# Gains moved out of the activations, and value and gate products in blocks of 512 columns, in a one-core encoder layer

## The chip, the cores and the metric

The kernel runs on one core of a Trainium2 chip. A core has engines that run side by side, each with its own stream of instructions in a fixed order: TensorE (PE in the profile; its weight loads are listed as PEld), VectorE (DVE), ScalarE (ACT), GpSimd (POOL) and SyncE (SP, which here only starts DMA transfers). Sixteen DMA engines move data between the chip's memory and the core's own memory. Products are accumulated in PSUM, in banks of 512 four-byte numbers for each of the 128 partitions.

The metric is the device time of one execution in microseconds, as the median of several runs. An instruction waits until the instructions ahead of it on its engine have been issued, and until what it reads is there and what it overwrites is no longer needed. So the order on an engine matters as much as the durations.

## The reference

One layer of a streaming encoder: a mixer made of three kinds of heads, then a feed-forward part with a causal convolution, each between two RMS norms. There are 1024 tokens of a new stream (the prompt) and 32 of a running one (the sample).

```python
def rms_norm(x, g):
    y = xf * lax.rsqrt(jnp.mean(xf * xf, axis=-1, keepdims=True) + EPS)
    return y * g

def head_rms_norm(x, g):
    y = x * lax.rsqrt(jnp.mean(x * x, axis=-1, keepdims=True) + EPS)
    return y * g.reshape(h, d)
...
proj = xn @ w_in           # 15 parts: queries, keys, decays; values gv, hi, mv; gates gr, hg, mo
o_a = head_rms_norm(o_a, g_a) * jax.nn.silu(hs(gr, GLA_H))
o_b = head_rms_norm(o_b, g_b) * jax.nn.silu(hs(hg, HG_H))
o_c = head_rms_norm(h, g_c) * jax.nn.sigmoid(hs(mo, ML_H))
cat = jnp.concatenate([o_a, o_b, o_c])
return cat @ w_out
...
h = mixer(rms_norm(x, g_mix_pre))      # the first of the two gains in question
x = x + rms_norm(h, g_mix_post)
h = conv_ffn(rms_norm(x, g_ffn_pre))
x = x + rms_norm(h, g_ffn_post)
```

Two gains matter here: `g_mix_pre`, one number for each of the 1024 features that enter `w_in`, and `g_head` (cut into `g_a`, `g_b`, `g_c`), one number for each of the 1024 features that enter `w_out`.

## The kernel before

**Work.** The tokens go in three groups: 384, 384, and 256 prompt plus 32 sample tokens. Within a group they are cut into units of 128 (the sample tokens are a short unit). A group passes through the projections (`inproj`). The head computations of a group (`mixer`, one unit after the other: levels of decays `x`, `Ld`, `Qz`, scores `sc`, outputs `og`, `oh`) are interleaved with the projections of the next group. After the third group come the output product (`zp`, blocks of 512 columns), the up product (`pux`, `puw`, `puy`, `puz`), and the down product (`q`, `x`). The order of instructions on each engine comes from a scheduler that simulates the program when the kernel is built; the code only gives the program order and a few constraints (`issue_after`, `high_priority`).

**Precision.** Each float32 operand of a product is split in a high part (a cast: `xh`, `wt_0h`) and a low part (the rest: `xl`, `wt_0l`), and one product is three matmuls, `mm3` (L101 high by high, L102, L103).

**Into the group.** `scale_x` takes each unit's rows `x` and multiplies them on DVE with the rstd of the row and with `gx`, the gain `g_mix_pre` copied to all partitions (512 KB; L310 for the two halves of the first unit, L319). `norm_group` transposes a unit on PE in two halves of four 128-column pieces into one PSUM tile `xt` each (L330). ACT casts a half out of PSUM into `xh` (L333), DVE subtracts to make `xl` (L334).

**Order of the projections in a group.** First block 0 of the values together with 26 columns of small gates: 282 columns, `pv` of block 0, each unit 24 matmuls; then the feature-major products `pf` (13 blocks of weights `wf_8`, `wf_6`, `wf_7`, `wf_3`, ...); then the blocks 1 to 7 of values and gates, 256 columns each. For a block the weights come in two tiles `wt_0`, `wt_1` (three in block 0). In the first group the raw weights are split on the chip (ACT L107, DVE or POOL L110) and the low parts stored (`lf_d`, `lt_d`, L355). In the later groups the low parts are loaded (SP L347) and only the cast is made again (ACT L349). Weight tiles have three raw buffers, and four buffers for high and low parts.

**Out of a block.** `vg_store` copies values out of PSUM (ACT L431) and sends them to `v_d`. For gates ACT makes a tanh (L113, into `vth`, one buffer; in the third group `gth`, three), DVE combines it with the sum in PSUM (L440, L442), POOL multiplies by `gh`, the gain `g_head` on all partitions (512 KB loaded on SP's queue at L652, times 0.5 on DVE at L653; L444), and POOL sends the result to `g_d` (L445). The third group makes blocks 1 to 7 feature-major with 288 columns and transposes them back (`vg_across`).

**Output weights.** `out_weights` splits the eight tiles of `w_out` (a cast on ACT, a subtraction on DVE).

## Time and profile before

| what | before |
|---|---|
| median of 3 runs (lowest, highest) | 1357.33 us (1355.49, 1357.98) |
| span of the profiled execution | 1355.3 us |
| PE busy | 1310.8 us, 97% |
| PEld busy | 1196.7 us, 88% |
| DVE busy | 1025.2 us, 76% |
| ACT busy | 709.8 us, 52% |
| POOL busy | 317.6 us, 23% |

The profile gives the span of its execution, first to last instruction, and no separate time for that execution; the three runs lie 0.2 to 2.7 us above the span. Busy time counts an instruction from its start to its modelled end. Matmuls overlap in the array, so their busy times sum to more than the time in which they pass; the distance from start to start is what one costs. The groups list an instruction by line, engine and tile names, with the mean of one, and the idle time of its engine just ahead of it with what ended that. In the timeline a row is a run of like instructions with the start and the time they took. In tables of windows PEclk is the granted clock of TensorE as a share of full speed.

### The profile page before, as it was taken

The page shows a single profiled execution, that of the slowest core. Times are in us where ns is not written, and L with a number is a line of the kernel's source. Part 1 is how long each engine was busy: PE and PEld are TensorE (multiplying, and loading weights), DVE is VectorE, ACT ScalarE, POOL GpSimd, SP SyncE. Part 2 cuts the span into 40 slices and gives each one's busy share as a digit, 9 for nine tenths or more (in the row PEclk, how much of TensorE's full clock was granted, in tenths as well). Part 3 has the DMA queues.
Part 4 walks back from the last instruction along what each step waited for, and adds up shares of the span by engine and source line. Part 5 has one row for each costly group of instructions (what it writes and reads, how often), then busy time and mean ns, then how long its engine had stood idle before and what let it go on. Part 6 is the DMA issues. An engine that isn't in the chain of part 4 may idle for free.

```text
span 1355.3 us, 29229 instructions
## 1 busy us (share of the span) xinstructions
PE 1310.8 (97%) x11472; PEld 1196.7 (88%) x11472; DVE 1025.2 (76%) x1921; ACT 709.8 (52%) x1362; POOL 317.6 (23%) x530
## 2 busy tenths in 40 slices
PE   6999999999999999999999999999999999999997
PEld 5999889998888887767899999999999996678885
DVE  5795649768598678876998888888888876499566
ACT  5555556555574555435654554545554545454552
POOL 4532303135032254213211212111111110010005
PEclk9999999999998989989999999999999999999998
DMA  9799778886879963454315457536455239645435
GB/s 342 241 358 363 265 244 258 278 281 211 292 230 308 336 201 125 142 182 103 128 48 188 134 133 189 134 111 180 120 147 154 82 127 397 254 161 146 141 102 124
DMA packets 126881, 269.72 MB, mean 199 GB/s; under 512 B 24167, under 2 KB 59143, under 8 KB 126663
## 3 DMA queue, kind: packets, MB, share of 16 engines
q1 hardware_dynamic: 113111, 244.78, 53.2%
q0 software_dynamic: 9120, 18.62, 7.3%
q10 hardware_dynamic: 4512, 4.46, 1.0%
q8 instruction: 90, 1.47, 0.5%
q14 instruction: 48, 0.39, 0.1%
HBM read 206.72 MB, written 86.18 MB: 216 GB/s over the span
## 4 chain that ended last, share of the span: by engine, by line
PE 63%; DVE 5%; DMA 3%; ACT 3%; issue 2%; POOL 1%; SPq 0%; DVEq 0%; POOLq 0%; ACTq 0%
PE pux L103 5%; PE pux L102 5%; PE pux L101 5%; PE puw L101 3%; PE puw L103 3%; PE puw L102 3%; PE q L101 3%; PE q L102 3%; PE q L103 3%; PE x L101 2%; PE x L102 2%; PE x L103 2%; PE puz L103 2%; PE puz L101 2%; PE puz L102 2%
## 5 line engine op out<-in xcount | busy, mean ns | idle before, releaser
L1409 DVE SCALAR_TENSOR_TENSOR y<-uu,fconv_sb,y 128x1060 f32<-128x1060 f32 x88 | 116.2, 1320 | 36.8 <-ACT y L1407 36.2
L1345 ACT COPY c<-pux 128x272 f32<-128x272 f32 (+1 forms) x132 | 49.3, 375 | 50.5 <-PE pux L103 49.8
L1407 ACT ACTIVATE y<-uu,fconv_sb 128x1060 f32<-128x1060 f32 x44 | 56.1, 1275 | 8.5 <-POOL uu L1403 7.8
L101 PE MATMUL pv<-wt_0h,xh 128*128 128x256 f32 (+1 forms) x192 | 56.3, 293 | 3.6 <-DVE xl L334 1.6
L103 PE MATMUL zp<-woh,cl 128*128 128x512 f32 (+1 forms) x144 | 57.7, 401 | 1.5 <-DVE cl L1106 1.5
L1406 POOL COPY fhalo<-uu 128x2 f32<-128x2 f32 x44 | 16.6, 376 | 180.7 <-DVE uu L1350 180.6
L101 PE MATMUL zp<-woh,ch 128*128 128x512 f32 (+1 forms) x144 | 57.8, 410 | 0.8 <-ACT ch L1105 0.8
L102 PE MATMUL zp<-wol,ch 128*128 128x512 f32 (+1 forms) x144 | 57.9, 402 | 0.0
L103 PE MATMUL pv<-wt_1h,xl 128*128 128x256 f32 (+1 forms) x192 | 55.1, 287 | 0.0
L103 PE MATMUL pv<-wt_0h,xl 128*128 128x256 f32 (+1 forms) x192 | 55.0, 286 | 0.0
L102 PE MATMUL pv<-wt_0l,xh 128*128 128x256 f32 (+1 forms) x192 | 54.8, 286 | 0.0
L101 PE MATMUL pv<-wt_1h,xh 128*128 128x256 f32 (+1 forms) x192 | 54.7, 285 | 0.0
L102 PE MATMUL pv<-wt_1l,xh 128*128 128x256 f32 (+1 forms) x192 | 54.4, 283 | 0.0
L1585 POOL TENSOR_TENSOR gss<-gss 128x1 f32<-128x1 f32 (+1 forms) x9 | 8.2, 906 | 185.0 <-ACT gjk L1578 185.0
L221 POOL TENSOR_SCALAR hrs<-hss 128x5 f32<-128x5 f32 (+3 forms) x27 | 10.1, 375 | 176.5 <-DVE hss L1015 172.6
L831 DVE COPY_PREDICATED P<-masks_sb,sc 128x352 f32<-128x352 int32 (+3 forms) x53 | 37.9, 715 | 5.9 <-PE sc L744 5.0
L101 PEld LDWEIGHTS pv<-wt_0h,xh 128*128 128x128 f32 x192 | 36.4, 190 | 5.3 <-DVE xl L334 2.1
L1403 POOL COPY uu<-uu 128x2 f32<-128x2 f32 x44 | 28.0, 637 | 38.8 <-DVE uu L1350 37.8
L101 PEld LDWEIGHTS pv<-wt_1h,xh 128*128 128x128 f32 x192 | 36.2, 189 | 0.7 <-issue 0.6
L222 POOL TENSOR_TENSOR hrs<-hrs,mhalf 128x5 f32<-128x5 f32 (+3 forms) x27 | 36.2, 1341 | 2.2
L103 PEld LDWEIGHTS pv<-wt_0h,xl 128*128 128x128 f32 x192 | 36.5, 190 | 0.2
L102 PEld LDWEIGHTS pv<-wt_0l,xh 128*128 128x128 f32 x192 | 36.5, 190 | 0.1
(1743 smaller groups left out, 5321.0 us busy)
## 6 DMA issues: line engine op xcount, KB each, us to landing
wrP<-in_w_dn SPq DMA_DIRECT2D x27, 512.0 KB, 4.4
h_d<-y SPq DMA_DIRECT2D x22, 530.0 KB, 3.7
ht<-h_d SPq DMA_DIRECT2D x22, 530.0 KB, 10.5
wt_0r<-in_w_tok SPq DMA_DIRECT2D x21, 512.0 KB, 5.7
wt_1r<-in_w_tok SPq DMA_DIRECT2D x21, 512.0 KB, 6.3
ws_d<-in_w_dn POOLq DMA_DIRECT2D x20, 512.0 KB, 8.9
wrP<-ws_d SPq DMA_DIRECT2D x20, 512.0 KB, 4.0
wt_0l<-lt_d SPq DMA_DIRECT2D x14, 512.0 KB, 4.5
```

Of the source, the lines that this page charges most:

```text
L101: pe.matmul(ps, lh[0], rh[0], start=first, stop=False, **kw)
L102: pe.matmul(ps, lh[0], rh[1], start=False, stop=False, **kw)
L103: return pe.matmul(ps, lh[1], rh[0], start=False, stop=last, **kw)
L221: pool.tensor_scalar(out, ss, 1.0 / width, eps, op0=ALU.mult, op1=ALU.add)
L222: pool.tensor_tensor(out, out, mhalf[:n, :cols], op=ALU.pow)
L831: dve.copy_predicated(dst, mk.broadcast_to([n, 11, *mk.shape[2:]]), src)
L1345: kept[name] = act.copy(t, ps)
L1403: pool.tensor_copy(u[:, GAP_P:GAP_P + 2], u[:, GAP_S - 2:GAP_S])
L1406: behind["POOL"] = pool.tensor_copy(fhalo[:, j, :], u[:, NCOL - 2:NCOL])
L1407: act.activation(y, u, AF.Identity, scale=fconv[:, j, 2:3], bias=fconv[:, j, 3:4])
L1409: dve.scalar_tensor_tensor(y, uu[i][:, s:s + NCOL], fconv[:, j, s:s + 1], y, op0=ALU.mult, op1=ALU.add)
L1585: pool.tensor_tensor(ss[:n, 0:1], ss[:n, 2:3], ss[:n, 3:4], op=ALU.add)
```

## The change

- **Gain of the norm as columns.** The tile `gx` and its load go. A table `gin` of 128 by 2 by 8 numbers holds both gains by columns (8 KB, loaded on ACT's queue). Rows are multiplied by the rstd alone. After the transposes the feature lies on the partitions, so the gain is a number per partition there: for each 128-column piece ACT writes `xh` with `scale` and DVE writes `xl` with one instruction of two operations. A half that had one cast and one subtraction has four and four: 18 halves, 72 pieces.
- **Gain of the heads in the output weights.** The tile `gh`, its load and its multiplication by 0.5 go, and so do the 36 multiplications on POOL. The tanh, the combination with the PSUM sum, and the DMA to `g_d` use one tile. The casts and subtractions of `w_out` carry the gain times 0.5, in as many instructions as before.
- **Blocks of 512 columns.** In the first two groups the blocks 1 to 6 become three wide blocks (`WIDE`, numbered 1, 3 and 5) of 512 columns. A wide block has four weight tiles of two 128-row parts by 512 columns (512 KB as before). One unit's sum fills one bank. Block 7 stays at 256 columns. High and low weight tiles have five buffers instead of four. The tile out of PSUM, `vg`, is 512 columns with two buffers. The three units of two narrow blocks were 6 x 24 matmuls of 256 columns; they are now 3 x 24 of 512 columns.
- **Stored low parts.** They lie in the layout of the wide blocks (`lw_d`). The third group, whose blocks stay narrow, reads them for blocks 1 to 6 in two transfers of 256 KB with rows of 1 KB, where it had one of 512 KB with rows of 4 KB.

```diff
-    gx = p1.tile([128, 1024], F32, name="gx")
-    act.dma_start(gx, a["grows"][3:4, :].broadcast_to([128, 1024]))
+    gin = cp.tile([128, 2, 8], F32, name="gin_sb")
+    act.dma_start(gin, a["gin"])
+    gmix, ghead = gin[:, 0], gin[:, 1]
...
-                dve.scalar_tensor_tensor(x[:n], x[:n], rs[:n], gx[:n], op0=ALU.mult, op1=ALU.mult)
+                dve.tensor_scalar(x[:n], x[:n], rs[:n], None, op0=ALU.mult)
...
-                s = slice(4 * hf, 4 * hf + 4), slice(off, off + n)
                 with tc.high_priority(offset=AHEAD):
-                    act.copy(xh[(slice(None), *s)], ps[:, :, :n])
-                    dve.tensor_tensor(xl[(slice(None), *s)], ps[:, :, :n], xh[(slice(None), *s)].bitcast(F32), op=ALU.subtract)
+                    for k in range(4):
+                        c, gk = (slice(None), 4 * hf + k, slice(off, off + n)), gmix[:, 4 * hf + k:4 * hf + k + 1]
+                        act.activation(xh[c], ps[:, k, :n], AF.Copy, scale=gk)
+                        dve.scalar_tensor_tensor(xl[c], ps[:, k, :n], gk, xh[c].bitcast(F32), op0=ALU.mult, op1=ALU.subtract)
...
-    def weights(src, pool_, name, shape, tags=("wr", "wh", "wl"), bufs=(3, 4), ...
+    def weights(src, pool_, name, shape, tags=("wr", "wh", "wl"), bufs=(3, 5), ...
...
+            elif blk in WIDE and g < 2:
+                parts = [(a["w_wide"][blk // 2, c], range(2 * c, 2 * c + 2), lw_d[blk // 2, c], 512) for c in range(4)]
...
-            pool.tensor_tensor(o[:n], th[:n], gh[:n, c0:c0 + 256], op=ALU.mult)
-            pool.dma_start(g_d[t:t + n, c0:c0 + 256], o[:n])
+            pool.dma_start(g_d[t:t + n, c1:c1 + w], th)
...
-            N = 256 if blk else 282
+            N = 512 if blk in WIDE else 256 if blk else 282
...
                         mm3(ps[:n, :N], (xh[:, k, off:off + n], xl[:, k, off:off + n]), ws[k], k == 0, k == 7)
+                        if k == 3 and N == 512:
+                            yield
...
-        if g == 0:
-            sp.dma_start(gh, a["grows"][2:3, :].broadcast_to([128, 1024]))
-            dve.tensor_scalar(gh, gh, 0.5, None, op0=ALU.mult)
...
-        for blk in range(1, 8):
+        for blk in (*WIDE, 7):
             yield from vg(blk)
-            if blk == 2 and g < 2:
+            if blk == 1 and g < 2:
                 for (u, off, n) in units_of(g + 1):
                     x_in[u] = load_x(u)
...
+            act.activation(W[1][k], wo_raw[k], AF.Copy, scale=gk)
+            dve.scalar_tensor_tensor(W[2][k], wo_raw[k], gk, W[1][k].bitcast(F32), op0=ALU.mult, op1=ALU.subtract)
```

The scheduler makes a new order from this. Three places follow. In the names of these rows the first digit after a tile's name is the unit or the group: `xt20` and `xt21` are the halves of the third unit, `pv2_0` the sum of the third unit in block 0, `wf0_6r` a raw weight tile of the first group.

The first is ACT at the start of the program, from the cast of `wf_8` on, before:

```order
L107 CAST wf0_8h_349<-wf0_8r_347 128x1024
L333 CAST xh0_162<-xt20_289 128x4x128
L460 COPY tgs0_180<-pv1_0_260 128x26
L431 COPY vg1_0_286<-pv1_0_260 128x256
L333 CAST xh0_162<-xt21_296 128x4x128
L107 CAST wf0_6h_407<-wf0_6r_405 128x1024
L460 COPY tgs0_180<-pv2_0_303 128x26
L431 COPY vg2_0_329<-pv2_0_303 128x256
L107 CAST wf0_7h_445<-wf0_7r_443 128x1024
```

And now, the same place (the pieces of the second unit, `xt10` and `xt11`, stand behind the cast of `wf_8`):

```order
L108 CAST wf0_8h_386<-wf0_8r_384 128x1024
L336 ACTIVATE xh0_163<-xt10_259,gin_sb_95 128x128 x2
L108 CAST wf0_6h_442<-wf0_6r_440 128x1024
...
L336 ACTIVATE xh0_163<-xt20_314,gin_sb_95 128x128
L108 CAST wf0_7h_480<-wf0_7r_478 128x1024
L336 ACTIVATE xh0_163<-xt21_327,gin_sb_95 128x128
L108 CAST wf0_3h_518<-wf0_3r_516 128x1024
L336 ACTIVATE xh0_163<-xt21_327,gin_sb_95 128x128
L476 COPY tgs0_181<-pv2_0_340 128x26
```

Before, one half of the third unit stood behind the cast of `wf_8` and none behind those of `wf_6`, `wf_7` and `wf_3`; now pieces of the second unit stand behind `wf_8` and `wf_6`, and the last two pieces of the third unit behind `wf_7` and `wf_3`.

The second is DVE where the first group's units enter the second group's projections: `xl1` is the second group's low part, `xt30` and `xt31` the halves of its first unit; `x0`, `Ld0`, `Qz0`, `kw2`, `w0`, `P` belong to the first unit's mixer. Before:

```order
L334 TENSOR_TENSOR xl1_1709<-xt30_1711,xh1_1708 128x4x128
L865 TENSOR_TENSOR Qz0_152<-x0_8_2177,qe0_1955 128x128
L442 TENSOR_SCALAR vth2_7_1695<-vth2_7_1695 128x256
L831 COPY_PREDICATED P_161<-masks_sb_110,sc0_2_2090 128x176x2
L856 TENSOR_TENSOR Ld0_150<-x0_8_2177,k0_1816 128x32x8
L334 TENSOR_TENSOR xl1_1709<-xt31_1718,xh1_1708 128x4x128
```

Now:

```order
L337 SCALAR_TENSOR_TENSOR xl1_1471<-xt30_1473,gin_sb_95,xh1_1470 128x128
L867 TENSOR_TENSOR Ld0_152<-x0_2_1869,k0_1602 128x128x2
L872 TENSOR_TENSOR Qz0_154<-x0_2_1869,q0_1601 128x128
L457 TENSOR_SCALAR vg2_1792_1458<-vg2_1792_1458 128x256
L862 TENSOR_TENSOR x0_8_1975<-b0_1603 128x512
L842 COPY_PREDICATED P_162<-masks_sb_111,sc0_0_1778 128x22x16
L337 SCALAR_TENSOR_TENSOR xl1_1471<-xt31_1486,gin_sb_95,xh1_1470 128x128
L862 TENSOR_TENSOR x0_4_1983<-b0_1603 128x512
L337 SCALAR_TENSOR_TENSOR xl1_1471<-xt30_1473,gin_sb_95,xh1_1470 128x128
L967 TENSOR_TENSOR x0_0_1991<-q0_1601,k0_1602 128x512
L337 SCALAR_TENSOR_TENSOR xl1_1471<-xt31_1486,gin_sb_95,xh1_1470 128x128
L867 TENSOR_TENSOR Ld1_153<-x0_4_1983,k0_1602 128x64x4
```

Two subtractions with four rows between them have become eight pieces with 19 rows of mixer work between the first and the last (the rows shown hold the first four).

The third is SP's queue in the second group, where raw and low weights of the values and gates are asked for (`wt1_3_1l`: second group, block 3, tile 1, low). Before, two tiles a block:

```order
L347 DMA wt1_4_1l_3512<-lt_d_90 128x1024
L343 DMA wt1_5_1r_3647<-in_w_tok 128x1024
L343 DMA wt1_6_0r_3991<-in_w_tok 128x1024
L767 DMA vm0_158<-v_d_81 128x5x64
L773 DMA ab3_4443<-a_d_79 64x320 x2
L347 DMA wt1_5_0l_3644<-lt_d_90 128x1024
L343 DMA wt1_6_1r_3997<-in_w_tok 128x1024
L347 DMA wt1_5_1l_3650<-lt_d_90 128x1024
```

Now, four tiles a wide block:

```order
L354 DMA wt1_3_1l_3092<-lw_d_91 128x1024
L354 DMA wt1_3_2l_3098<-lw_d_91 128x1024
L346 DMA wt1_5_0r_3271<-in_w_wide 128x1024
L354 DMA wt1_3_3l_3104<-lw_d_91 128x1024
...
L354 DMA wt1_5_1l_3280<-lw_d_91 128x1024
L354 DMA wt1_5_2l_3286<-lw_d_91 128x1024
L346 DMA wt1_7_0r_3694<-in_w_tok 128x1024
L354 DMA wt1_5_3l_3292<-lw_d_91 128x1024
```

A block of the weights is still asked for tile by tile, but with five buffers and four tiles a block only one tile of the next block finds a free buffer while a block is in use; the others wait until the last unit has passed the part that held the buffer.

More of the change, by code (lines that the diff above doesn't have):

```diff
@@ L346, in weights @@
         if kept:
-            behind["low"] = sp.dma_start(l.bitcast(F32), low.bitcast(F32))
+            if len(low.shape) > 3:
+                for c in range(2):
+                    behind["low"] = sp.dma_start(l[:, 2 * c:2 * c + 2].bitcast(F32), low[c].bitcast(F32))
+            else:
+                behind["low"] = sp.dma_start(l.bitcast(F32), low.bitcast(F32))
             if heng is None:
@@ L460, in vg @@
                     act.copy(tgs[:n, i, :], ps[:n, 256:])
-                vg_store(blk, u, off, n, ps)
+                vg_store(256 * blk, N if blk else 256, u, off, n, ps)
                 yield
```

74 lines of the change are left out of this document (40 added, 34 removed).

## The prediction

> **What bounds the kernel now.** I read the page first, then PE's waits, then the timeline of PE, ACT, DVE and SP at the three places where the change acts, then windows with the clock.
>
> ```profile
> span 1355.3 us, 29229 instructions
> PE 1310.8 (97%) x11472; PEld 1196.7 (88%) x11472; DVE 1025.2 (76%) x1921; ACT 709.8 (52%) x1362; POOL 317.6 (23%) x530
> PE xt L330 <- DVE x L310: 9.7, 1, 9.7
> PE pv L101 <- DVE xl L334: 1.6, 2, 1.4
> PE pv L101 <- DVE vth L440: 1.5, 1, 1.5
> PE pv L103 <- DMA wt_1l<-lt_d: 1.2, 1, 1.2
> ```
>
> PE is the bound: 97% busy. Of the waits that the change touches (the last four rows: waited for, us in total, times, longest), the first is the start, before any data is there; the other three sum to 4.3 us. So a gain can come from matmuls that pass faster, from a shorter start, or from these few waits. POOL is 23% busy, and what it no longer does counts only where somebody waits for it.
>
> What a matmul costs is its distance to the next one, read from the timeline between the first and last row of an unbroken stretch. The first pair stands 45 matmuls of 256 columns apart, the second 12 matmuls of 512 columns.
>
> ```profile
> 94.72 0.28 PE L101 MATMUL pv<-wt_0h,xh 128*128 128x256 f32 x1
> 99.94 0.28 PE L103 MATMUL pv<-wt_0h,xl 128*128 128x256 f32 x1
> 565.08 0.39 PE L103 MATMUL zp<-woh,cl 128*128 128x512 f32 x1
> 567.81 0.39 PE L103 MATMUL zp<-woh,cl 128*128 128x512 f32 x1
> L101 PE MATMUL pv<-wt_0h,xh 128*128 128x256 f32 (+1 forms) x192 | 56.3, 293 | 3.6 <-DVE xl L334 1.6
> L103 PE MATMUL zp<-woh,cl 128*128 128x512 f32 (+1 forms) x144 | 57.7, 401 | 1.5 <-DVE cl L1106 1.5
> ```
>
> (99.94 - 94.72) / 45 = 0.116 us for 256 columns, (567.81 - 565.08) / 12 = 0.2275 us for 512. Two narrow ones cost 0.232.
>
> **Wider blocks.** Two groups, three units, three wide blocks, 24 matmuls each: 432 wide ones for 864 narrow. 432 x (0.232 - 0.2275) = 1.9 us gained. Bounds: nothing, and 4 us if a narrow one is 0.1185 in slower stretches. I take -2. The weight loads halve too, but they lie beside the matmuls (PEld overlaps PE), so I count nothing for them; in an unbroken stretch the distance of 0.116 holds what they cost. The section "Back-to-back issue gap" of the Trainium skill's page "TensorE: Matmul & The Clock Gate" gives an isolated spacing of N / 2.4 + 2.5 ns, by which 432 fixed parts of 2.5 ns go, an estimate of 1.1 us instead of my 1.9.
>
> **The start.** The rows of ACT and SP there, and of DVE and ACT for the pieces' prices:
>
> ```profile
> 12.11 0.59 ACT L333 CAST xh<-xt 128x512 fp32r<-128x512 f32 x1
> 17.46 0.19 ACT L460 COPY tgs<-pv 128x26 f32<-128x26 f32 x1
> 20.25 1.05 ACT L107 CAST wf_8h<-wf_8r 128x1024 fp32r<-128x1024 f32 x1 [2.02 <-DMA wf_8r<-in_w_feat]
> 21.67 0.18 ACT L460 COPY tgs<-pv 128x26 f32<-128x26 f32 x1
> 24.58 1.05 ACT L107 CAST wf_6h<-wf_6r 128x1024 fp32r<-128x1024 f32 x1 [1.96 <-DMA wf_6r<-in_w_feat]
> 26.48 0.18 ACT L460 COPY tgs<-pv 128x26 f32<-128x26 f32 x1 [0.86 <-PE pv L103]
> 24.20 0.38 SPq L343 DMA_DIRECT2D wf_3r<-in_w_feat  x1
> DMA to landing us min/median/max: 5.8/5.8/5.8
> 21.30:26.30 5.00, 4.56 (x42) 3.85 (x40) 2.02 (x3) 2.37 (x5) 2.90 (x2) 1.00 1.04 419
> L1210 ACT ACTIVATE xg<-fxt,gcols_sb x8: 362/384/411, 646.6 to 648.4; 128x128 f32<-128x128 f32 x8
> L861 DVE TENSOR_TENSOR Qz<-x,q x53: 174/279/981, 114.1 to 591.4; 128x128 f32<-128x128 f32 x48, 128x32 f32<-128x32 f32 x5
> L334 DVE TENSOR_TENSOR xl<-xt,xh x18: 284/688/714, 11.4 to 344.7; 128x512 fp32r<-128x512 f32 x16, 128x128 fp32r<-128x128 f32 x2
> ```
>
> The landing row is that of `wf_3r` in the first group. The copies `tgs` at 17.46, 21.67 and 26.48 mark the ends of the three units of block 0. The windows row (PE, PEld, DVE, ACT, POOL busy, clock, DMA share, GB/s) shows the DMA engines full while PE still works: loads are what the features wait for here.
>
> Loads first: 1 MB less is written (`gx`, `gh`). At the 419 GB/s of the windows row that is about 2.5 us by the time `wf_6r` comes, 1.2 us of it ahead of the first unit. So `wf_8r` can land near 17.7, `wf_6r` near 22, each instead of the cast's start at 20.25 and 24.58.
>
> Then the pieces. A half by four activations like `xg` (the only ones here out of PSUM with a scale per partition) takes 8 in 646.6 to 648.4, so about 0.26 us from start to start, 1.0 a half against 0.5 to 0.6 for the cast. On DVE I take 0.28 for a piece by the 128x128 row, 1.1 a half against 0.69. First unit: ACT now has all three weight casts ahead, then the eight pieces with the Square of the third unit between; `xl` likewise has three splits ahead and the third unit's scaling between. I put the last `xl` near 16.5, by ten of these instructions behind the loads, and the unit's end near 18, about half a microsecond later than 17.5 even with data 1.2 us sooner.
>
> Second unit: all eight `xh` pieces stand behind `wf_8`'s cast (18.7), the last six behind that of `wf_6` too (23): 23 + 0.2 for the copy + 6 x 0.26 + 0.3 for the last `xl` gives 25.1, then what matmuls are left, 26. Before, this unit was done when ACT copied its sum at 21.7. Third unit: the last two pieces stand behind the casts of `wf_7` and of `wf_3`. Before, `wf_3r` was asked for at 24.20, behind POOL's split of `wf_8`; now that split is 1.6 us sooner at the best, so `wf_3r` lands near 22.6 + 5.8 = 28.4, its cast ends at 29.4, the last piece, its `xl` and six matmuls end near 30.5. Before it was 26.3. That is +4. The features then follow PE-bound as they did, and I see no cover for this: every later matmul needs them. Bounds: -1.2 if the pieces wait for none of the casts' loads (data sooner and nothing else), +6.5 if loads are no sooner than before (then `wf_3r` lands at 30, third unit near 32.5).
>
> **First to second group.** Rows of PE, of windows (the last is the stretch in which the first new unit's halves come and its matmuls pass), and of DVE's, POOL's and ACT's groups.
>
> ```profile
> 142.63 0.58 PE L101 MATMUL pv<-wt_0h,xh 128*128 128x256 f32 x1 [1.53 <-DVE vth L440]
> 142.60:146.00 3.40, 3.37 (x15) 3.37 (x16) 3.28 (x11) 1.97 (x6) 1.45 (x2) 0.51 0.53 207
> 146.00:149.40 3.40, 3.40 (x44) 3.20 (x44) 1.78 (x8) 2.25 (x7) 1.62 (x2) 0.99 0.33 97
> L851 DVE TENSOR_TENSOR x<-b x44: 272/680/1362, 108.9 to 582.6; 128x512 f32<-128x512 f32 x40, 128x128 f32<-128x128 f32 x4
> L831 DVE COPY_PREDICATED P<-masks_sb,sc x53: 332/553/985, 145.5 to 599.2; 128x352 f32<-128x352 int32 x40, 128x704 f32<-128x704 int32 x8, 32x176 f32<-32x176 int32 x4, 32x352 f32<-32x352 int32 x1
> 153.25:160.07 6.82, 6.52 (x75) 5.80 (x72) 6.76 (x15) 3.63 (x10) 1.63 (x4) 1.00 0.98 362
> L444 POOL TENSOR_TENSOR vg<-vth,gh x24: 717/732/1656, 118.8 to 334.1; 128x256 f32<-128x256 f32 x24
> ACT vth L113: 11.7, 7
> ```
>
> Now: PE waits 1.5 us for a gate's `vth`, and right behind it the clock is at 0.51 for 3.4 us: 15 matmuls where the next window has 44. So a wait of 1.5 us cost about 1.5 + 1.7. That wait hangs on one buffer of `vth`, held until POOL's L444 has read it (0.73 us; ACT waited 11.7 us in 7 places for it). L444 is gone and there are two buffers: up to 3.2 us gained. A page rule bears on the clock: the Trainium skill ("TensorE: Matmul & The Clock Gate", "Part 1: The HAM clock gate") says that the clock halves after an idle window of about 3.4 us. The length of the slow stretch agrees; here 1.5 us of idling was enough to start one.
>
> Against it stands DVE's order. Between the first and last `xl` piece of the new unit 19 rows of mixer work now stand: 22 instructions: three level products like L851 (0.68), three `P` (L831, 0.55) and 16 others, which I take at the 0.28 of L861, the row nearest in size: 2.0 + 1.7 + 4.5 = 8.2 us, and 2 us of pieces. Each matmul group of that unit waits for its piece, and PE's order has only about 3 us of block 0 and 3 us of mixer products to put there. So 4 to 5 us idle where the stretch from 153.25 to 160.07 had 6.82 - 6.52 = 0.3, but the same mixer work is then done earlier, and I give back a third: 3 us of idling, and one slow stretch (1.7) as before. Sum 3 + 1.7 - 3.2 - 0.3 = +1.2; I take +1.5, bounds -3 (wait and slow stretch go, pieces hidden) and +5 (5 us idle and a second slow stretch).
>
> **Second to third group.** There the chain is a gate, then the transposes, then `xh` and `xl`:
>
> ```profile
> 328.98 0.66 PE L330 MATMUL xt<-ident,x 128*128 128x128 f32 x4 [0.73 <-ACT vth L113]
> 332.75 0.40 PE L101 MATMUL pv<-wt_0h,xh 128*128 128x282 f32 x1 [1.39 <-DVE xl L334]
> ```
>
> The 0.73 goes with L444; the 1.39 grows by twice (1.05 - 0.6) on ACT at the most. I take +0.5, bounds -2 and +3.
>
> **Weights of the wide blocks.** One tile of the next block finds a buffer; part j + 1 waits until the third unit has passed part j. Its user comes one unit later: 24 x 0.2275 = 5.5 us.
>
> ```profile
> SPq L347 <- PE pv L103: 33.5, 18, 6.0
> DMA to landing us min/median/max: 4.9/6.5/8.7
> ```
>
> The landing row is that of `wt_1l`. A release to landing of 4.9 to 8.7 against 5.5, and SP waits for releases already (33.5 us), with loads for the mixers queued behind on SP. Twelve such tiles' low parts come in the second group's wide blocks; three of them are first parts with room. If half of the nine others wait 0.5 us, PE loses 2; mixer products stand between and cover part. In the first group nothing is loaded twice, but DVE splits four tiles instead of two at a time, the same 1024 columns each. I take +1 for both, bounds 0 and +5.
>
> **Third group and the output weights.** The chain that ended last runs through POOL there:
>
> ```profile
> 494.69 0.72 POOL vg L444
> 496.31 1.42 POOL vg L444 x2
> 498.25 5.91 DMA g_d<-vg
> ```
>
> L444 goes from it: 2.1 us off a chain whose far end PE only partly waits for. Take -1, bounds 0 and -3. Low parts in 1 KB rows: twelve more issues on SP of about 0.4 us (as `wf_3r`'s 0.38), beside PE's work; if that cover is gone, one issue, 0.4, delays the last tile. The casts of `w_out` keep their count and sizes; I count nothing. On DVE the scaling gets cheaper, `gh`'s product goes, the pieces cost 18 x 0.4 more: even. ACT gets 18 x 0.5 = 9 us more at 52% busy, hidden except in the places above.
>
> Sum: -2 + 4 + 1.5 + 0.5 + 1 - 1 = +4 us. The profiled span of 1355.3 becomes 1359.3; the median of the runs is 2.0 over this span, so 1361.3.
>
> **Rivals.** (a) *Faster, by the gates and the earlier data.* Place: the start and 141 us. If the casts `wf_6`, `wf_7`, `wf_3` never hold pieces back (their loads come over 2 us sooner than I have it), the start gains 1.2 instead of losing 4, and the wait at 141 with its slow stretch is not replaced: -2 - 1.2 - 3 - 1 + 1 = -6, 1351. For it: DMA is full at the start and 1 MB goes. Against it: the order puts the last piece behind `wf_3`, which was cast only far behind the third unit before. It decides as soon as that cast starts before 25.
> (b) *Slower still, by releases.* The low parts come late for half the blocks (+5), and two more stretches at half clock follow (2 x 1.7), on top of the start: 1361.3 + 4 + 3.4 = 1369. For it: the 33.5 us that SP waits. Against: it waits without PE waiting now, but for 1.2 us.
> (c) *No net change.* Pieces cost at the start about what is gained in the clock: 1357.
> (d) *Wide matmuls are much cheaper.* By the mean durations of the groups, 2 x 0.293 - 0.401 = 0.185 us would go with each, 80 us in all: 1277. Overlapping ends are not time: `zp`'s own distance of 0.2275 speaks against it. In the same section on the issue gap the Trainium skill has a sustained 131 ns for 512 columns. As a mechanism of this kernel that would be a wide stream that passes at less than half of `zp`'s distance, 432 x (0.232 - 0.131) = 44 us, 1313 by an estimate from that figure; no row of 512 columns here shows it.
>
> **How the numbers follow.** My case (start held by the casts, within 2.7 and 10 us slower) 0.44; (b) 0.08; (c) 0.21; (a) 0.26; (d) 0.01. The runs lie within 0.2%, 2.7 us, which is what a measurement can tell from no change. Faster: (a) and (d), 0.27. Same: (c), 0.21. Slower: 0.52. The range from 1348 to 1371 takes in (a)'s bounds (the start at -1.2, the transition at -3, the third group at -3) and most of (b). My case's own range is 1360 to 1367.
>
> **What would show it.** Right: the copy `tgs` of the third unit starts near 30.5 instead of 26.48, with `xh` pieces just behind the casts of `wf_7` and `wf_3`; 512-column `pv` rows 0.2275 apart; near 140 to 160 PE waits of a few tenths to 1 us for `xl`; no wait for `vth`; SP waits on `pv` at the low loads. Wrong: the features start at 26 or before, no half clock near 141, or matmuls of 512 columns that stand closer than 0.22.

## The result and the profile after

The change made the kernel slower: 1394.97 us median of 4 runs (1387.85 to 1402.72) against 1356.94 us before (4 runs, 1355.49 to 1357.98). The ratio is 1.0291, 95% interval [1.025, 1.0332]: 38 us where +4 was forecast, outside the range. The profiled execution is the shortest of the four, so its 30.7 us over the span before are the lower end of what there is to explain. (One run of the kernel before, beside a later experiment, took 3210.9 us and stands in no ratio.)

The head of the page of the changed kernel:

```profile
span 1386.0 us, 28413 instructions
PE 1322.2 (95%) x11040; PEld 1174.8 (85%) x11040; DVE 1025.7 (74%) x1969; ACT 721.0 (52%) x1404; POOL 286.3 (21%) x488
```

PE is no less the bound, but idles more: 63.8 us against 44.5. These 19 us are the larger part of the 30.7; the rest is booked as busy PE. The mean granted clock of the span is 0.983 in both profiles, so the sum of slow stretches does not tell the two executions apart. The place is found by cutting the span where the transposes `xt` of a group begin and where its first feature product `pf` begins. Between the two stands block 0, in which each unit's rows are transposed, split and multiplied. The windows of these three stretches, of the kernel before (columns: length, busy PE, PEld, DVE, ACT, POOL with counts, PEclk, DMA share, GB/s; the first window includes the start):

```profile
0.00:26.30 26.30, 15.81 (x109) 13.96 (x110) 15.65 (x34) 13.42 (x25) 11.11 (x25) 1.00 0.92 322
150.90:169.10 18.20, 17.90 (x226) 15.69 (x225) 9.99 (x21) 9.18 (x20) 3.66 (x6) 1.00 0.91 306
327.60:349.00 21.40, 19.07 (x257) 15.64 (x257) 17.32 (x48) 13.97 (x36) 8.02 (x11) 1.00 0.54 173
```

And of the changed kernel:

```profile
0.00:32.70 32.70, 19.41 (x108) 16.31 (x109) 18.26 (x52) 19.82 (x45) 13.00 (x26) 1.00 0.90 312
152.90:185.30 32.40, 30.00 (x432) 23.47 (x430) 20.47 (x61) 18.35 (x52) 1.35 (x3) 1.00 0.63 214
334.40:377.50 43.10, 35.72 (x460) 28.05 (x458) 28.99 (x87) 19.82 (x57) 6.01 (x10) 0.80 0.43 137
```

The stretches grew by 6.4, 14.2 and 21.7 us. In the second and third more mixer matmuls run (432 against 226 and 460 against 257 PE records), so part of that comes back in the features behind them, which take 64.8 instead of 71.7 and 55.1 instead of 61.1 us. In the third the clock is at 0.80 on the mean.

So the growth of a stretch is not yet lost time. What is lost shows in how far a kernel lies behind the kernel before when the same work begins, in us, from the timelines (the kernels of the lower three rows are those of the experiments below):

| kernel | first transpose, second group | first transpose, third group | first output product | first up product | end of the span |
|---|---|---|---|---|---|
| changed | 2.0 | 6.8 | 25.9 | 34.9 | 30.7 |
| narrow blocks, alternating pieces | 1.6 | 7.3 | 22.5 | 23.6 | 19.3 |
| wide blocks, pieces in two loops | 0.9 | 8.0 | 21.8 | 21.4 | 17.6 |
| narrow blocks, pieces in two loops | -0.7 | -0.1 | 1.4 | 4.9 | 2.3 |

The first group gives nearly all of its 6.4 us back. Most is lost in the third group, between its first transpose and the first output product: 19.1 us.

What holds block 0 up is seen in the timeline of ACT and DVE in the first stretch, second unit:

```profile
24.90 0.37 ACT L336 ACTIVATE xh<-xt,gin_sb 128x128 fp32r<-128x128 f32 x1 [0.42 <-DVE xl L337]
25.30 0.35 DVE L337 SCALAR_TENSOR_TENSOR xl<-xt,gin_sb,xh 128x128 fp32r<-128x128 f32 x1 [0.44 <-ACT xh L336]
25.69 0.88 ACT L336 ACTIVATE xh<-xt,gin_sb 128x128 fp32r<-128x128 f32 x2 [0.42 <-DVE xl L337]
26.09 0.35 DVE L337 SCALAR_TENSOR_TENSOR xl<-xt,gin_sb,xh 128x128 fp32r<-128x128 f32 x1 [0.44 <-ACT xh L336]
```

The pieces do not run side by side. ACT makes one, DVE waits 0.44 for it and makes its own, ACT waits 0.42 for that before it makes the next: 25.69 - 24.90 = 0.79 us a piece, 3.2 us a half where before a cast of 0.59 and a subtraction of 0.69 did. In the waits of the whole span (waited for, us, times, longest) the two engines stand for each other:

```profile
ACT xh L336 <- DVE xl L337: 13.0, 22, 2.0
DVE xl L337 <- ACT xh L336: 15.2, 21, 3.5
```

In the built program an ACT piece carries a wait on DVE unless it is the first of its tile `xt`: the order of the code (ACT, DVE, ACT, DVE on one PSUM tile) has become an order between the engines. Whether the chip needs that wait was not tried.

0.79 us is the round when nothing else stands between. In the second and third group it does: each engine takes its instructions in order, so an ACT piece waits until DVE has come through the mixer work ahead of its own piece, and the other way round. Between the first and last of a group's 24 pieces stand 19 other instructions on ACT and 28 on DVE in the second group, 28 and 48 in the third. From the first `xh` piece to the end of the last `xl` piece this takes 24.9 and 36.1 us, where the casts and subtractions of the kernel before took 13.0 and 13.6.

The copies `tgs` at the ends of the first group's units now:

```profile
22.21 0.17 ACT L476 COPY tgs<-pv 128x26 f32<-128x26 f32 x1
27.25 0.17 ACT L476 COPY tgs<-pv 128x26 f32<-128x26 f32 x1
30.71 1.05 ACT L108 CAST wf_3h<-wf_3r 128x1024 fp32r<-128x1024 f32 x1
31.66 0.36 ACT L336 ACTIVATE xh<-xt,gin_sb 128x128 fp32r<-128x128 f32 x1
32.90 0.18 ACT L476 COPY tgs<-pv 128x26 f32<-128x26 f32 x1 [0.88 <-PE pv L104]
```

The last piece of the third unit does stand behind the cast of `wf_3`, as read from the order, but that cast itself is behind pieces now, and did not wait for its load; it holds the piece by its own 1.05 us.

The wide matmuls, an unbroken stretch of 18 from the first to the last row:

```profile
103.69 0.39 PE L102 MATMUL pv<-wt_3h,xh 128*128 128x512 f32 x1
107.90 0.40 PE L102 MATMUL pv<-wt_2h,xh 128*128 128x512 f32 x1
```

(107.90 - 103.69) / 18 = 0.234 us. The prediction's two rows of 256 columns lie 44 matmuls apart in the timeline, not 45, so one costs (99.94 - 94.72) / 44 = 0.1186 us and two cost 0.237. A wide one gains about 0.003 us, 1.4 us for all 432.

### The profile page after: what moved, and what is told of

The parts are those of the page before. It is cut to its first block, busy times and chain, and to the rows that moved or that the text cites. A ratio compares the mean times of both kernels' runs of the same rounds, so it can differ in the third digit from the quotient of the medians.

```text
span 1386.0 us, 28413 instructions
## 1 busy us (share of the span) xinstructions
PE 1322.2 (95%) x11040; PEld 1174.8 (85%) x11040; DVE 1025.7 (74%) x1969; ACT 721.0 (52%) x1404; POOL 286.3 (21%) x488
## 4 chain that ended last, share of the span: by engine, by line
PE 75%; DVE 8%; DMA 6%; ACT 6%; issue 3%; POOL 1%; SPq 1%; DVEq 0%; ACTq 0%; POOLq 0%
PE pux L103 4%; PE pux L102 4%; PE pux L104 4%; PE pv L102 4%; PE pv L104 4%; PE pv L103 3%; PE puw L102 3%; PE puw L103 3%; PE puw L104 3%; PE q L102 3%; PE q L103 3%; PE q L104 3%; PE x L102 2%; PE x L103 2%; PE pf L102 2%
## 5 line engine op out<-in xcount | busy, mean ns | idle before, releaser
L1414 POOL COPY fhalo<-uu 128x2 f32<-128x2 f32 x44 | 16.6, 377 | 177.7 <-DVE uu L1358 177.7
L1030 POOL TENSOR_TENSOR cat<-cat,gt 128x320 f32<-128x320 f32 (+3 forms) x27 | 35.4, 1311 | 26.2 <-DVE cat L1028 26.0
L755 PEld LDWEIGHTS sc<-Qz,Ld 64*64 64x64 f32 (+2 forms) x1344 | 25.6, 135 | 14.1 <-issue 6.4
L102 PEld LDWEIGHTS zp<-woh,ch 128*128 128x128 f32 (+1 forms) x144 | 27.1, 188 | 11.9 <-DVE z L1220 3.2
L755 PE MATMUL sc<-Qz,Ld 64*64 64x32 f32 (+5 forms) x1344 | 30.7, 223 | 5.8 <-DVE Qz L876 4.5
L1026 DVE TENSOR_REDUCE hss<-sq 128x5 f32<-128x320 f32 (+3 forms) x27 | 13.6, 503 | 28.9 <-ACT sq L1025 28.8
L102 PE MATMUL pv<-wt_0h,xh 128*128 128x512 f32 (+3 forms) x84 | 30.6, 364 | 4.7 <-ACT vg L446 1.9
L336 ACT ACTIVATE xh<-xt,gin_sb 128x128 fp32r<-128x128 f32 (+1 forms) x72 | 24.0, 357 | 20.7 <-DVE xl L337 13.0
L104 PEld LDWEIGHTS zp<-woh,cl 128*128 128x128 f32 (+1 forms) x144 | 27.0, 187 | 8.7 <-issue 1.2
L337 DVE SCALAR_TENSOR_TENSOR xl<-xt,gin_sb,xh 128x128 fp32r<-128x128 f32 (+1 forms) x72 | 22.9, 334 | 15.4 <-ACT xh L336 15.2
L103 PEld LDWEIGHTS zp<-wol,ch 128*128 128x128 f32 (+1 forms) x144 | 26.8, 186 | 7.1 <-issue 0.8
```

The source lines that it names most:

```text
L102: pe.matmul(ps, lh[0], rh[0], start=first, stop=False, **kw)
L103: pe.matmul(ps, lh[0], rh[1], start=False, stop=False, **kw)
L104: return pe.matmul(ps, lh[1], rh[0], start=False, stop=last, **kw)
L336: act.activation(xh[c], ps[:, k, :n], AF.Copy, scale=gk)
L755: line[0] = fn(*args, **kw)
L1030: pool.tensor_tensor(cat[:n, c0:c0 + 64 * nh], cat[:n, c0:c0 + 64 * nh], gt[:n, c0:c0 + 64 * nh], op=ALU.mult)
```

## The experiments

All ratios are to the kernel before, run on the same chip in the same session. Differences between kernels are taken between their ratios, times 1356 us.

**First, one part at a time.** Theory 1: the hand-over on one `xt` tile. Theory 2: the pieces' number and time. Theory 3: buffers and low weights of the wide blocks.

*Pieces in two loops:* the changed kernel with

```diff
-                    for k in range(4):
-                        act.activation(xh[c], ps[:, k, :n], AF.Copy, scale=gk)
-                        dve.scalar_tensor_tensor(xl[c], ps[:, k, :n], gk, xh[c], ...)
+                    for k in range(4):
+                        act.activation(xh[c], ps[:, k, :n], AF.Copy, scale=gk)
+                    for k in range(4):
+                        dve.scalar_tensor_tensor(xl[c], ps[:, k, :n], gk, xh[c], ...)
```

> All 72 + 72 pieces stay, with their sizes and gains; only the code's order changes: the four ACT pieces of a half are written first, then the four DVE pieces, so that no ACT piece waits for a DVE piece of the same xt tile. Theory 1 (the hand-over ACT to DVE to ACT on one xt tile, about 0.79 us a round, holds up block 0 in all three groups): 1350 to 1362 us, block 0 of the first group ends before 28. Theory 2 (the pieces are too many and too long as such): 1380 or more. Theory 3 (late buffers and low weights of the wide blocks): 1380 or more.

Measured: 1372.62, ratio 1.0122 [1.0097, 1.0148], against 1.0291 with the same instructions alternating. No theory had this number: theory 1 is right for 23 us and does not explain the other 16. Now eight pieces run through, the first four of one tile `xt`, the others of the next. ACT goes on to the second tile while DVE has not begun on the first, so it is the tile `xt`, and not `xh`, that orders the engines:

```profile
10.28 2.16 ACT L336 ACTIVATE xh<-xt,gin_sb 128x128 fp32r<-128x128 f32 x8
12.31 1.12 DVE L338 SCALAR_TENSOR_TENSOR xl<-xt,gin_sb,xh 128x128 fp32r<-128x128 f32 x4
13.42 1.12 DVE L338 SCALAR_TENSOR_TENSOR xl<-xt,gin_sb,xh 128x128 fp32r<-128x128 f32 x4
```

2.16 us for eight on ACT and 1.12 for four on DVE: the prices that the prediction had taken (0.26 and 0.28).

*Halves again, wide blocks kept:* one cast and one subtraction a half, without the gain.

```diff
-                    for k in range(4): ...
+                    act.copy(xh[s], ps[:, :, :n])
+                    dve.tensor_tensor(xl[s], ps[:, :, :n], xh[s], op=ALU.subtract)
```

> The changed kernel with one cast and one subtraction a half again; the gain of the norm is left out of the computation. Wide blocks and the gain of the heads in the output weights stay. Theory 1: within 3 us of the kernel with the pieces in two loops, 1349 to 1360. Theory 2: 1349 to 1360 too, but 20 us or more under the kernel with two loops. Theory 3: 1380 or more.

Measured: 1373.85, ratio 1.0142 [1.0117, 1.0168]. The same as with pieces in two loops: 54 more instructions on each engine cost nothing that can be measured. Theory 2 falls.

*Narrow blocks, pieces alternating:*

```diff
-WIDE = (1, 3, 5)
+WIDE = ()
-def weights(..., bufs=(3, 5), ...)
+def weights(..., bufs=(3, 4), ...)
-mx.tile([128, 512], F32, tag="vg", bufs=2)
+mx.tile([128, 256], F32, tag="vg", bufs=3)
```

> The changed kernel with narrow blocks again (256 columns, two weight tiles a block, four buffers); the pieces alternate between ACT and DVE as in the change. Theory 1 and theory 2: still slow, 1378 to 1402. Theory 3: back at 1353 to 1363.

Measured: 1375.77, ratio 1.0143 [1.0108, 1.0178]. That lies in no theory's range. Half of the loss goes with the wide blocks. So there are two causes, of about equal size, and each theory alone was too simple. The granted clock has its part here: in the third group's block 0 of this kernel (42.3 us) it is 0.64 on the mean, while PE idles only 2.6 us.

*The gain of the heads alone:* the kernel above with `gx` and the halves back.

> The kernel before with one part of the change, the gain of the heads in the output weights (no multiplication on POOL, no load of 512 KB for it). All three theories: 1350 to 1358, the wait for the gate's tile near 141 us gone; what it gains is what this part alone is worth.

Measured: 1353.64, ratio 0.999 [0.9974, 1.0007]. By the ratio this part is worth 1.4 us; the interval, from 3.5 us faster to 0.9 slower, takes in nothing at all. What it was to remove at 141 us is gone, as the windows of this kernel show:

```profile
139.40:146.00 6.60, 6.60 (x58) 6.60 (x58) 5.52 (x15) 5.18 (x13) 3.77 (x7) 1.00 0.93 292
```

PE is busy throughout and the clock full, where the kernel before waited 1.5 us and then ran 3.4 us at 0.51.

**Second, the pieces without the wide blocks, and where the wide blocks cost.**

*Narrow blocks, two loops* (both edits shown above):

> Narrow blocks, the gain of the heads in the output weights, and the gain of the norm by pieces in two loops (no ACT piece waits for DVE). Theory 1 (the hand-over was the whole cost of the pieces): as with the gain on rows, 1348 to 1357; the pieces' own time is hidden. Theory 2 (pieces cost by number): 1360 or more.

Measured: 1356.56, ratio 1.0007 [0.9987, 1.0028], against 1.0143 with the pieces alternating. The gain as columns costs nothing that can be told from noise if the code does not alternate the engines. The stretches of block 0, from the first transpose to the first feature product, in us:

| kernel | first group | second | third |
|---|---|---|---|
| before | 16.6 | 18.1 | 21.3 |
| narrow, gain on rows | 18.3 | 18.4 | 20.0 |
| narrow, two loops | 18.4 | 20.2 | 23.6 |
| narrow, alternating | 22.7 | 30.7 | 42.3 |
| changed (wide, alternating) | 24.7 | 32.4 | 43.1 |
| wide, two loops | 17.5 | 25.4 | 25.1 |

*Wide blocks that leave PSUM in 256 columns:* theory A blames the two buffers `vg`, for which ACT, and behind it PE, waits in the kernel with two loops:

```profile
ACT vg L114 <- DMA g_d<-vg: 6.5, 1, 6.5
PE pv L102 <- ACT vg L114: 5.7, 2, 5.2
```

```diff
-mx.tile([128, 512], F32, tag="vg", bufs=2)
+mx.tile([128, 256], F32, tag="vg", bufs=4)
-vg_store(256 * blk, N if blk else 256, u, off, n, ps)
+for h in range(max(N // 256, 1)):
+    vg_store(256 * blk + 256 * h, 256, u, off, n, ps[:, 256 * h:256 * h + 256])
```

> Two loops and wide blocks, but a unit's 512 columns leave PSUM in two tiles of 256 columns out of four buffers, with a transfer each (the same memory as two buffers of 512). Theory A (the two buffers out of PSUM, held until the transfer has landed, make the wide blocks slow): 1355 to 1366, and the wait of PE for the gate's tile at the passage to the third group, 5.2 us, is gone. Theory B (four weight tiles to five buffers) or theory C (the scheduler's other order of the mixer steps): 1368 or more.

Measured: 1371.18, ratio 1.0123 [1.0102, 1.0143]. That 5.2 us wait is gone, and the time is the same: theory A falls.

*Wide blocks in one group alone* (the width of a sum and the loop over the blocks change with it):

```diff
-elif blk in WIDE and g < 2:
+elif blk in WIDE and g in (0,):        # the other kernel: (1,)
```

> Two loops, wide blocks in the first group alone; the second group has narrow blocks, with five buffers. Theory A: the gates of the second group leave in 256 columns, so most goes, 1352 to 1362. Theory B: the low parts are loaded in the second group, so most goes as well, 1352 to 1362; the first group costs at most 4. Theory C: cost splits between the groups, 1360 to 1368.

> Two loops, wide blocks in the second group alone. Theories A and B: most of the cost stays, 1364 to 1374. Theory C: 1360 to 1368, about as much as with the first group alone.

Measured: 1381.29, ratio 1.0188 [1.0167, 1.0209], and 1377.39, ratio 1.0163 [1.0142, 1.0184]. Each alone costs at least as much as both together. That fits none of the theories; in both kernels the narrow blocks had to live with two `vg` buffers and five weight buffers, so the pair says little on the place, and nothing on what passing a wide block costs.

**Third, buffers.** Theory B: weight tiles get a buffer late. Theory C: the scheduler's other order of mixer steps.

*Narrow blocks with three and with five buffers:*

```diff
-def weights(..., bufs=(3, 4), ...)
+def weights(..., bufs=(3, 3), ...)     # the other kernel: (3, 5)
```

> Narrow blocks, two loops, with three buffers for high and for low weights instead of four: a block of two tiles has one tile of the next ahead of it, as a wide block has one of four. Theory B (tiles ask for a buffer late; SP stands in line on releases, raw weights come late, and ACT's casts hold up what is behind them): 1366 or more, with SP's waits for releases up by 20 us or more. Theory C (the order of the mixer steps with wide blocks): within 4 us of the kernel with four buffers, 1352 to 1361.

> The same with five buffers. Theory B: 0 to 4 us faster than with four (1352 to 1357), since four already hold a whole block ahead. Theory C: within 3 us of four.

Measured: 1374.52, ratio 1.0142 [1.0116, 1.0168], with three, and 1374.65, ratio 1.016 [1.0135, 1.0185], with five. Three is late supply, as theory B had it: SP's waits for PE's releases at the low loads rise from 55.0 to 75.5 us, and PE waits 13.4 us in all for low parts, against 1.1 us with four. The longest row of that kernel:

```profile
PE pv L104 <- DMA wt_1l<-lt_d: 6.8, 3, 4.9
```

Five I had expected to be harmless. They cost 21 us, with narrow blocks. ACT's waits with five buffers in the stretch from 100 to 150 us, the first five groups (a wait is put down to what came last, so a cast that stands there can be listed under another transfer):

```profile
ACT wt_1h L108 <- DMA k<-qkb_d: 3.2, 1, 3.2
ACT wt_1h L108 <- DMA wt_1r<-in_w_tok: 3.1, 1, 3.1
ACT wt_1h L108 <- PE pv L104: 3.1, 1, 3.1
ACT wt_1h L108 <- DMA mqk_d<-y: 2.4, 1, 2.4
ACT wt_0h L108 <- DMA wt_0r<-in_w_tok: 2.3, 2, 1.9
```

With four buffers, the casts' waits there:

```profile
ACT wt_1h L108 <- DMA wt_1r<-in_w_tok: 4.6, 3, 2.1
ACT wt_0h L108 <- DMA wt_0r<-in_w_tok: 1.9, 1, 1.9
```

The five rows sum to 14.1 us, the two to 6.5. With the smaller rows of the casts as well, ACT stands at them for 16.8 us with five buffers and 10.0 with four, and a part of that ends with PE's products and not with a load. This made theory D: with a buffer more the scheduler puts a cast earlier in ACT's order than its load lands, and the gates' tanh and all else on ACT stand behind it.

*Low loads of the wide blocks on ACT's queue:*

```diff
-behind["low"] = sp.dma_start(l, low)
+behind["low"] = (act if shape[1] == 2 else sp).dma_start(l, low)
```

> Wide blocks, two loops, 256-column tiles out of PSUM; the loads of the low parts in the second group are asked for on ACT's queue instead of SP's, so SP no longer stands on releases ahead of the raw loads. Theory B: 5 us or more faster than the 1371 of this kernel with SP's queue. Theory C: 1368 to 1375.

Measured: 1368.67, ratio 1.0102 [1.0072, 1.0131], 3 us under the same kernel with SP's queue, and the intervals overlap. Not decided, and at most a small part.

**Fourth.** The changes to the wide ones are to the kernel with 256-column tiles out of PSUM, those to the narrow ones to the kernel with two loops.

*Wide with four weight buffers:* `bufs=(3, 4)`.

> Wide blocks, two loops, 256-column tiles out of PSUM, with four weight buffers instead of five: no tile of the next block can be loaded ahead. Theory B (late release): 10 us or more slower than with five, 1381 or more. Theory D (the fifth buffer lets ACT's casts stand in its order ahead of loads that have not landed, and ACT stands): 1357 to 1368. Theory E (the order with four buffers and narrow blocks is a lucky one, any other costs 10 to 20): 1366 to 1380.

Measured: 1383.33, ratio 1.0203 [1.0174, 1.0233]. The fifth buffer is worth 11 us to wide blocks, the size that theory B had said. Its mechanism is not shown by that: PE waits 0.7 us for low parts in this kernel, and at the first output product it is only 2.0 us behind the kernel with five. The rest comes between there and the first up product (170.2 us against 158.2), behind the last value and gate block.

*Casts held back, narrow with five buffers and wide:*

```diff
+with tc.issue_after(held[0].ins):     # ACT's drain of the block before's first unit
     act.copy(h, r)
```

> Narrow blocks, two loops, five buffers; the casts of a block's weights may not stand on ACT ahead of the drain of the block before's first unit, one narrow block less a unit ahead of their use. Theory D: most of the 18 us that the fifth buffer cost goes, 1354 to 1364. Theory E: 1366 to 1380.

> Wide blocks, two loops, 256-column tiles out of PSUM, five buffers, casts held in the same way. Theory D: 5 us or more under the 1371 without it, 1355 to 1366. Theory B and theory E: 1367 to 1378.

Measured: narrow 1363.21, ratio 1.0059 [1.0036, 1.0082]; wide 1377.17, ratio 1.0158 [1.0137, 1.0179]. In the narrow kernel holding the casts takes back 14 of the 21 us of the fifth buffer, as theory D forecast. The only wait left at such a cast on ACT from 100 to 150 us:

```profile
ACT wt_1h L363 <- DMA wt_1r<-in_w_tok: 2.8, 2, 2.2
```

Yet theory D is not shown. Where ACT stood at the casts, in the first group, the five buffers had lost 6.1 us to the kernel with four by the second group's first transpose, and holding the casts gave back 1.1 of them. Of the 18 us between the two profiled spans, 10 lie between the first output product and the first up product (172.8 us against 162.5), where these casts are long done. The edit also made another order of the mixer steps, and no run takes the two apart.

In the wide kernel holding the casts takes nothing back. Theory D is not what the wide blocks suffer from, or not in a way that this edit removes.

*Another pace:* narrow, `NIN` 40 instead of 38.

> Narrow blocks, two loops, four buffers; the code's pace of mixer steps beside the projections is 40 steps instead of 38, a change that means nothing by itself. It leaves half of PE's order as it was. Theory E: 1364 to 1376. Theories B and D: 1353 to 1361, as without it.

Measured: 1353.78, ratio 0.9991 [0.998, 1.0002]. Half of PE's order is another and the time is the same, so it is not so that any new order costs 15 us. Theory E falls.

*More buffers for the wide blocks:* a pair without the low parts of the activations.

```diff
-xl = p1.tile([128, 8, T], F32R, tag="xl")
+xl = xh                                # DVE's pieces go back to PSUM
-def weights(..., bufs=(3, 5), ...)
+def weights(..., bufs=(3, 6), ...)     # the second of the pair
```

> The control of the next kernel: wide blocks, two loops, 256-column tiles out of PSUM, five weight buffers; the tile of low parts of the activations is left out to free memory (its DVE pieces are written back to PSUM, its matmuls read the high parts; as many instructions and matmuls). All theories: 1364 to 1374.

> The same with six weight buffers instead of five, two tiles of the next wide block ahead. Theory B (late release): 4 us or more under the control, after the 12 us from four to five. Theory D (casts ahead of their loads): as the control or slower.

Measured: 1378.87, ratio 1.0166 [1.0143, 1.0188], and 1375.15, ratio 1.0151 [1.012, 1.0182]. The control came out above its expectation, and the sixth buffer gives 2 us with overlapping intervals: not settled, and no second step of 11.

*Mixer steps forward in the wide kernel:* `NIN` 34. The reason was this stretch, the third group's features, in the wide kernel and in the narrow one with two loops:

```profile
352.40:426.00 73.60, 66.54 (x826) 61.09 (x825) 56.66 (x145) 43.09 (x97) 13.38 (x22) 0.93 0.79 254
```

```profile
351.10:412.00 60.90, 58.85 (x744) 54.85 (x743) 47.87 (x122) 40.57 (x90) 12.46 (x19) 1.00 0.85 282
```

> Wide blocks, two loops, 256-column tiles out of PSUM, five buffers, with the mixer steps written at a pace of 34 steps instead of 38, so earlier in the code. Theory F (with wide blocks the mixer steps come late in the second group and run where PE waits for them in the third): 5 us or more under the 1371 without it. Otherwise 1368 to 1376.

Measured: 1383.46, ratio 1.0218 [1.0179, 1.0256]: 13 us worse. Theory F's forecast fails. The edit did act where it was aimed: from the third group's first feature product to the first output product this kernel takes 151.5 us instead of 164.6. It loses more elsewhere, 7.7 us of it between the first output product and the first up product.

**What stays open.** With the pieces in two loops, the wide blocks cost 16 us (1.0122 and 1.0123 against 1.0007). Shown is that they are 11 us slower without the fifth buffer, that a fifth buffer by itself costs narrow blocks 21 us, and that the edits to the `vg` buffers, to SP's queue, to the casts' place and to the mixers' pace do not bring the 16 us back. What carries them was not found. The traces narrow the place: most of it shows in the third group, from its first feature product to the first output product, where the blocks are narrow in both kernels. The wide kernel with 256-column tiles out of PSUM, and the narrow one with two loops:

```profile
352.40:517.00 164.60, 150.64 (x2010) 138.31 (x2008) 114.57 (x313) 87.69 (x209) 37.89 (x59) 0.94 0.78 255
351.10:499.80 148.70, 142.06 (x1928) 130.88 (x1926) 109.56 (x296) 86.39 (x204) 36.99 (x56) 0.98 0.83 278
```

Six of the other kernels with wide blocks and no alternating pieces take 158.4 to 161.6 us there, the rest 151.5 (the pace of 34) to 156.8; the four narrow ones with four buffers and no alternating pieces take 147.7 to 149.5. PE's waits there are mostly for the mixers' work on DVE and ACT. So the order of the mixer steps (theory C) may carry the 16 us; it was never ruled out, and it was not shown. A rival stands untested: every wide kernel reads the third group's low parts in rows of 1 KB, every narrow one in rows of 4 KB. In the changed kernel, in the wide one above and in the wide one with two loops PE waits for none of these loads, which speaks against it.

No kernel tried was faster than the kernel before by more than its interval; narrow ones with the heads' gain in the output weights, or with the pace of 40 as well as two loops, lie at 0.999 and end at 1.0007 and 1.0002.

## Why the prediction was wrong, point by point

**Direction right, size wrong by a factor of more than nine.** Slower was the likelier side, from the right place (block 0's pieces), but with +4 for +38.

**The pieces at the start (+4) and at the two transitions (+1.5, +0.5): the step that failed.** The prediction took 0.26 us a piece on ACT and 0.28 on DVE and let the engines run beside each other. Both durations were right, as the two loops show; the sentence "a half by four activations ... 1.0 a half ... on DVE ... 1.1 a half" left out that the second ACT piece waits for the first DVE piece. One round is 0.79 us, a half 3.2, and more where mixer work stands between the pieces. The three stretches grew by 6.4, 14.2 and 21.7 us. Set against the terms of +4, +1.5 and +0.5, the changed kernel had lost 2.0 us by the second group's first transpose, 4.8 more by the third's, and 19.1 more by the first output product (the wide blocks' share included): the passage to the third group, priced at twice 0.45 us on ACT, is the term that failed most. In whole runs alternating costs 18 to 23 us (1.0143 against 1.0007 narrow, 1.0291 against 1.0122 wide). At the start the casts `wf_6`, `wf_7` and `wf_3` were thought to hold the pieces by their loads. In the changed kernel the casts of `wf_7` and `wf_3` waited for no load. With two loops the first features begin at 25.7, 0.6 earlier than before; that does not clear the casts, because the order changed too, and the third unit's pieces now go ahead of all three:

```profile
21.55 1.18 ACT L336 ACTIVATE xh<-xt,gin_sb 128x128 fp32r<-128x128 f32 x4
23.20 1.05 ACT L108 CAST wf_6h<-wf_6r 128x1024 fp32r<-128x1024 f32 x1 [0.46 <-DMA wf_6r<-in_w_feat]
```

The order of instructions, quoted ahead of the prediction, showed the result of this chain (eight pieces strewn among 19 rows of mixer work), and it was read as other work put first. Pieces that stand apart can also mean that the next one was not free to go, and here it was that.

**Weights of the wide blocks (+1, bounds 0 and +5): wrong in size.** Wide blocks as a whole cost 16 us, beyond the bound, and the cause is open. The mechanism named (one tile ahead, release late, PE waiting for low parts) is not borne out: PE waits for no low part of a wide block in the changed kernel, and for 0.7 us with four buffers. Most of the loss shows in the third group, which the term did not look at.

**Wider blocks (-2): nearly right, by two errors that cancel.** The narrow distance is 0.1186 us, not 0.116, because the rows lie 44 steps apart; the wide one is 0.234, not 0.2275, which came from the output product, a stream of other operands. 432 x (0.237 - 0.234) is some 1.4 us gained where 1.9 was forecast; that is luck. Rival (d) is refuted: 512 columns cost 0.234 us, within 2% of two narrow ones.

**Heads' gain in the output weights (-1, and the wait at 141): right.** The wait and its slow stretch are gone in the kernel with that part alone, and the whole is worth -1.4 us by the ratio, not told from nothing.

**Loads in 1 KB rows, `w_out`'s casts:** counted at nothing; no run here takes them apart. The issue of such a load on SP has a median of 0.54 to 0.56 us in the wide kernel with 256-column tiles, against the 0.4 taken.

**Rivals.** (b), slower by releases, 1369, was the nearest in number; its price was for a few late tiles, which PE did not wait for, and no rival had the chain between two engines. Several of the signs named for "right" came all the same: the third unit's copy starts at 32.90, with pieces behind the casts of `wf_7` and `wf_3`, and PE waits 0.7 us at the longest for `xl` in the second group's block 0. They showed slower pieces, not why. And the runs of the kernel before later spread over up to 0.7%, so the 2.7 us taken for what a measurement can tell was too narrow.

## What to carry to other kernels

When one tile is read piece by piece by two engines, write all pieces of the first engine and then all of the second: alternating code became alternating engines, and 0.26 us a piece became 0.79, or more where either engine had other work in between. Before pricing small pieces, ask the built program what each piece waits for; a duration says nothing of a hand-over. And a buffer more is not free where a scheduler sets the order: it moves other instructions too, and here cost the narrow kernel 21 us. A stretch that grows may only do work earlier, so look for the loss where the same work starts late.

## What the runs showed that was not expected

- Runs of the changed kernel spread over 1.1% (1387.85 to 1402.72) where the kernel before spreads over 0.2% beside it (up to 0.7% in the other sessions). The mean granted clock goes roughly with it: 0.983, 0.976, 0.978 and 0.970 for 1387.85, 1394.27, 1395.67 and 1402.72 us. Which waits set off the slow stretches of the longer runs is not known, since only the shortest has a trace.
- The distance of matmuls of 512 columns depends on the stream: 0.234 us in `pv`, 0.2275 in `zp`, at full clock in both.
